# Squares of x summed in PSUM, Sin and Tanh emitted elsewhere, and the first merge weights loaded ahead of x

## The chip, the cores and the metric

The kernel runs on one core of a Trainium2 chip. The metric is the device time of one execution in microseconds, as a median of runs. TensorE (PE) multiplies matrices and has its weight loads listed apart (PEld), VectorE (DVE) does elementwise work, ScalarE (ACT) activations and copies, GpSimd (POOL) elementwise work too, and SyncE (SP) issues the DMA transfers. Each engine executes its own instructions in order.

## What is computed

One layer of an encoder over 1024 positions with 1024 channels, all in float32:

```
h    = rms_norm(x, g)
proj = h @ w_in                      # latent columns, RWKV columns, gate columns
o_a  = mla_branch(...)               # attention; rotary cos/sin of positions on q and k
o_b  = rwkv7_branch(...)             # uses tanh(low-rank decay columns), sigmoid(...)
x    = x + (sig(gA) * (o_a @ w_o[:512]) + sig(gB) * (o_b @ w_o[512:])) @ w_merge
x    = x + gated_mlp(rms_norm(x))
```

What the change touches is the root mean square of `x` over its channels, `cos` and `sin` of `positions * frequency`, the `tanh` of the two decay columns, and the product with `w_merge` together with the addition of `x` behind it.

## The kernel before

Everything is held transposed: 128 channels on the partitions, 1024 positions along the free axis, two halves of 512 (`HT`). A float32 product is made of three products in a reduced type: each operand is split into a high part (a cast on ACT) and a low part (a subtraction on DVE or POOL), and high x high, high x low and low x high are added in PSUM. `mmk` (L295) emits these six products, three for each half; this is called a step. `split` (L211) makes the parts of a weight tile: the cast `whi` on ACT, the subtraction `wlo` on POOL.

**The order of work.** The instructions of TensorE stand in the order in which the program emits them (L248). For DVE, ACT, POOL and SP, in the first part and around the merge, a scheduler of the language chooses the order from its own model of time; program order counts as priority. `act` (L152) adds ordering edges so that ScalarE's table sets are loaded in the order of emission: Ln and Exp share a set, Sigmoid and Tanh share one, Sin has its own.

**The start (L304 to L405).** `XORDER` (L42) lists the steps of the start: "w" loads and splits half of a weight tile of one of the first three projections (two for the latent q, one for the latent kv), "x" loads one of eight row blocks of x (`ld`, L322: hh on ACT, hl on DVE), "m" is one step of product, "q" squares a row block (`square`, L328: Square on ACT in place, then an addition into `acc` on POOL), "r" makes the rotary tables (`rotary_tables`, L340), and "s" sums the squares over the partitions with a product of `acc` by ones and takes the reciprocal root `rstd` by Ln and Exp on ACT. In TensorE's order "s" stands behind the two q products and ahead of the last four steps of the kv product. The rotary tables are 17 DVE instructions over 128 x 1024 and two Sin on ACT; they use the tiles `ang`, `kq`, `sinT` and `cosT`. `evac` (L400) then multiplies the three results by `rstd`, which empties their PSUM banks.

**The projections behind it (L436 to L761).** `inproj` emits eight steps of one projection and calls `done` behind the last. The first two are l2 and l1 (L752). `shift` (L449) evacuates one into the single tile `u` and mixes each position with its neighbours (Identity on ACT, two DVE instructions); then `l1_done` and `l2_done` (L703, L707) apply Tanh to one half of the tile. Two lanes of background work (L719) are woven between the steps: generators such as `norm_ckv` and `norm_cq` (normalisations, L480), `key_rope` (L507, with the sum rsk), `mla_nope` and `rw_prep` (L637, for each of four pairs: three low-rank products from l1 and l2 with a Sigmoid behind each half). A generator that yields a key goes on after so many estimated nanoseconds of TensorE work as `DELAY` (L57) says for it, so this table sets where its products stand in TensorE's order.

**The merge (L1659 to L1733).** After the branches are mixed, the eight row blocks of x are loaded into `x2[j]` (L1659), held by an ordering edge behind the last gate load. Then, for each j, `product` (L1377) takes two weight tiles of 512 columns of `w_merge[j]`, from the list `first` if it holds any and otherwise by a load at that place, and makes eight steps; `residual` (L1709) adds `x2[j]`, and several ACT and DVE instructions scale, split and square the sum. Raw weight tiles, high parts and low parts have two buffers each.

Of the kernel before, what the change touches and what calls it, by code (L numbers as in the profile page):

```python
# [10 lines left out]
F32 = mybir.dt.float32  # L11
R = mybir.dt.float32r
I32 = mybir.dt.int32
# [41 lines left out]
CARRY = 3000  # L55
BATCH = 2500
DELAY = {  # L57
    "tab": 2100, "sum": 3900, "cq": 2040, "kr": 3100, "kr2": 750, "kr3": 0, "nope": 2975, "nope2": 1440,
    "rope": 541, "rope2": 5334, "rope3": 1470, "v": 805, "lora": 746, "kk": 10600, "kk2": 1785, "rk": 4080,
    "bo": 400,  # L60
}
# [25 lines left out]
def block_kernel(ctx: ExitStack, tc: tile.TileContext, a):  # L87
# [44 lines left out]
    def pool(name, bufs=1, side="left", space=bass.MemoryType.SB):  # L132
        return tc.tile_pool(name=name, bufs=bufs, side=side, space=space, reuse_waits="tile")
# [137 lines left out]
    onef = ap_.tile([128, 128], F32, name="onef")  # L271
    G.memset(onef, 1.0)
    G.tensor_copy(onesr, onef)
    HT = (slice(0, 512), slice(512, 1024))

    nst = [0]
# [27 lines left out]
    cqps = [big(), big()]  # L304
    ckps = [up1(), up1()]
    first3 = [*cqps, ckps]
    with pool("xp") as xp:
        xt = [xp.tile([128, T], F32, name=f"xt{k}") for k in range(8)]
        acc = xp.tile([128, T], F32, name="xacc")
        w3 = {}  # L310

        def wl3(t, h):
            raw = xp.tile([128, 512], F32, tag=f"raw{t}", name=f"raw{t}{h}")
            nc.sync.dma_start(raw, a["w_in"][t][:, h * 512:(h + 1) * 512])
            if h == 0:
                hi, lo = (xp.tile([128, 512], R, name=f"{n}{t}") for n in ("whi", "wlo"))
            else:
                hi, lo = (wpool["w"].tile([128, 512], R, tag=n, name=n, bufs=2) for n in ("whi", "wlo"))
            split(raw, hi, lo)
            w3[t, h] = hi, lo  # L320

        def ld(k):  # L322
            nc.sync.dma_start(xt[k], a["xT"][k * 128:(k + 1) * 128, :])
            hh, hl = hx[k]
            S.activation(hh, xt[k], AF.Copy, scale=vc("gmix", k))
            V.scalar_tensor_tensor(out=hl, in0=xt[k], scalar=vc("gmix", k), in1=hh.bitcast(F32), op0=mult, op1=sub)

        def square(k):  # L328
            if k == 0:
                S.activation(acc, xt[0], AF.Square)  # L330
            else:
                S.activation(xt[k], xt[k], AF.Square)
                G.tensor_tensor(out=acc, in0=acc, in1=xt[k], op=add)

        def mm(t, k):
            wh, wl = w3[t, k // 4]
            ws = slice(k % 4 * 128, (k % 4 + 1) * 128)
            mmk(first3[t], wh[:, ws], wl[:, ws], hx[k], k == 0, k == 7)

        def rotary_tables():  # L340
            posi = xp.tile([128, T], I32, name="posi")
            nc.sync.dma_start(posi, a["pos"].to_broadcast([128, T]))
            ang, kq = (xp.tile([128, T], F32, name=n) for n in ("ang", "kq"))
            V.tensor_copy(ang, posi)
            V.tensor_scalar(ang, ang, cst[:, C_FREQ:C_FREQ + 1], None, op0=mult)
            magic = 12582912.0
            for dst, off, fin in ((sinT, 0.0, 0.0), (cosT, 0.25, 0.5 * math.pi)):
                V.tensor_scalar(kq, ang, 1.0 / (2 * math.pi), off, op0=mult, op1=add)
                V.tensor_scalar(kq, kq, magic, -magic, op0=add, op1=add)
                src = ang  # L350
                rest = 2 * math.pi
                for bits in (8, 8, 8, 24):
                    if bits == 24:
                        cc = float(np.float32(rest))
                    else:
                        m, e = math.frexp(rest)
                        cc = math.ldexp(math.floor(m * 2 ** bits), e - bits)
                    rest -= cc
                    V.scalar_tensor_tensor(out=dst, in0=kq, scalar=-cc, in1=src, op0=mult, op1=add)
                    src = dst  # L360
                pi_ = 3.1415925
                if fin:
                    V.tensor_scalar(dst, dst, fin, pi_, op0=add, op1=ALU.min)
                    V.tensor_scalar(dst, dst, -pi_, None, op0=ALU.max)
                else:
                    V.tensor_scalar(dst, dst, pi_, -pi_, op0=ALU.min, op1=ALU.max)
                act(dst, dst, AF.Sin)

        for step in XORDER:
            if step[0] == "w":  # L370
                wl3(step[1], step[2])
            elif step[0] == "x":
                ld(step[1])
            elif step[0] == "q":
                square(step[1])
            elif step[0] == "r":
                rotary_tables()
            elif step[0] == "m":
                mm(step[1], step[2])
            else:  # L380
                for hs in HT:
                    ss = ss1()
                    E.matmul(ss, onef, acc[:, hs], start=True, stop=True)
                    rsqrt_(rstd[:, hs], ss, 1.0 / D, eps)
# [9 lines left out]
    def keep(i, n, dtype=F32):  # L394
        return tt(n, RV[i], 1, dtype)
# [4 lines left out]
    def evac(q, ps):  # L400
        for x, hs in zip(ps, HT):
            V.tensor_tensor(out=q[:, hs], in0=x, in1=rstd[:, hs], op=mult)

    for q, ps in zip([*cqs, ckv], first3):
        evac(q, ps)  # L405

    nc.sync.dma_start(a2w, a["w_l1"])
    for dst, src in ((b64r, a["consts"][:, C_B64:]), (b16, a["b16"])):
# [40 lines left out]
    def shift(ps, i, out):  # L449
        u = tt("u", "u", 1)  # L450
        evac(u, ps)
        S.activation(out, u, AF.Identity, scale=c0[:, i:i + 1])
        V.scalar_tensor_tensor(out=out[:, 1:], in0=u[:, :-1], scalar=vc("mp", i), in1=out[:, 1:], op0=mult, op1=add)
        V.scalar_tensor_tensor(out=out[:, :-1], in0=u[:, 1:], scalar=vc("mn", i), in1=out[:, :-1], op0=mult, op1=add)
# [25 lines left out]
    def norm_cq():  # L480
        sq = [tt("sq") for _ in range(2)]
        for i in range(2):
            S.activation(sq[i], cqs[i], AF.Square)
        G.tensor_tensor(out=sq[0], in0=sq[0], in1=sq[1], op=add)
        pt = parted2(sq[0])
        yield "sum"
        rs = tt("rs")
        for x, hs in zip(pt, HT):
            rsqrt_(rs[:, hs], gsum(onesr, x), 1.0 / 256, eps)
        for i in range(2):  # L490
            V.scalar_tensor_tensor(out=cqs[i], in0=cqs[i], scalar=vc("gqa", i), in1=rs, op0=mult, op1=mult)
            split(cqs[i], cqh[:, i, :], cql[:, i, :], V)
        yield "cq"
# [143 lines left out]
    def rw_prep(p):  # L637
        cs = slice(p * 128, (p + 1) * 128)
        w2b = tp.tile([64, 128], F32, tag="w2b", name="w2b", bufs=2)
        nc.sync.dma_start(w2b, a["w_l2"][:, cs])  # L640
        at = keep(3, "at")
        for dst, wt, src, bias, key in (
            (at, a2w[0:64, cs], l1[0:64, :], vc("a0", p), None),
            (None, a2w[64:128, cs], l1[64:128, :], vc("w0f", p), "s0"),
            (None, w2b, l2[0:64, :], vc("w0b", p), "s1"),
        ):
            if dst is None:
                dst = tt("sg")
            for hs in HT:
                ps = up1()  # L650
                mul(ps, wt, src[:, hs], start=True, stop=True)
                act(dst[:, hs], ps, AF.Sigmoid, bias=bias)
                yield "lora"
            if key:
                nc.sync.dma_start(d_rw[key][:, p, :], dst)
# [46 lines left out]

    def l1_done(ps):  # L703
        shift(ps, 0, l1)
        act(l1[64:128, :], l1[64:128, :], AF.Tanh)

    def l2_done(ps):  # L707
        shift(ps, 1, l2)
        act(l2[0:64, :], l2[0:64, :], AF.Tanh)

    def gl_done(d):
        def done(ps):
# [943 lines left out]
    for j in range(2, 8):  # L1656
        for _ in mixture(j):
            pass
    for j in range(8):  # L1659
        i = nc.sync.dma_start(x2[j][:, :], a["xT"][j * 128:(j + 1) * 128, :])  # L1660
        tc.add_manual_dep(i.ins, fetched[0].ins.name, NOSYNC, reason="after the branch's operands")

# [48 lines left out]
    for j in range(7):  # L1713
        ps = big4()
        for _ in product(ps, a["w_merge"][j], yx):
            pass
        if j == 6:
            first.extend([wrows(a["w_merge"][7], k, 8) for k in (0, 4)])
        residual(j, ps)
        k, g = j % 4, vc("gffn", j)  # L1720
        y1, y2_ = ps
        scaled((B11 if j < 4 else B21)[k], y1, g)
        if j < 4:
            d = t5("p1")
            S.copy(d, y1)
            V.tensor_tensor(out=d, in0=y2_, in1=d, op=sub)
            scaled(U1[k], d, g)
        else:
            t3, t2 = sums(j, ps, scaled_b12(j))
            split(t3, *U3[k], V)  # L1730
            split(t2, *U2[k], V)
            scaled(B22[k], y2_, g)
        squares(j, ps)  # L1733
# [461 lines left out]
```

## Time and profile before

| | |
|---|---|
| median of 3 runs | 1922.2 us (1920.16 to 1922.29) |
| profiled execution | 1920.34 us |
| its span | 1918.4 us |
| mean granted TensorE clock | 0.978 |
| busy PE / DVE / ACT / POOL | 1832.6 / 1220.6 / 871.5 / 654.1 us |
| DMA | 210.65 MB, mean 110 GB/s |

Times in the profile count from the start of the span. A line of the timeline has start, duration, engine, line of the program, operation, output and inputs by tile name, shape, and how many instructions were put together; in brackets stands how long the engine had been idle and what released it. Nearly all instructions are recorded in two helpers (L108, and L123 for TensorE), so they are told apart by their tiles. The ends of products are modelled: where products follow each other closely, the distance between starts is what one takes.

### The profile page before, as it was taken

What the parts mean: (1) busy time and instruction counts of PE and PEld (TensorE: products, weight loads), DVE (VectorE), ACT (ScalarE), POOL (GpSimd) and SP (SyncE); (2) the same over time, 40 slices, a digit from 0 to 9 for tenths busy, and PEclk for the clock granted to TensorE, in tenths of its full rate; (3) what the DMA queues carried; (4) which work ended last, traced back from release to release, by engine and by line L of the source; (5) the groups of instructions that cost most, each with busy time, mean ns of one, the idle gap of its engine ahead of it and who ended that gap; (6) DMA issues with size and microseconds to landing.
All of it is one profiled execution on the core that took longest, in us unless ns stands there. A gap on an engine that the chain in (4) does not pass through costs nothing. (4 is left out here: it accounts for less than half of the span.)

```text
span 1918.4 us, 36770 instructions
## 1 busy us (share of the span) xinstructions
PE 1832.6 (96%) x14928; PEld 1464.1 (76%) x14928; DVE 1220.6 (64%) x1853; ACT 871.5 (45%) x1390; POOL 654.1 (34%) x566
## 2 busy tenths in 40 slices
PE   6889999999999998998999999999999999999998
PEld 5657676888788776776777877877888888888886
DVE  7567665445466586776673363697666766667667
ACT  5576577223232565665666543543323323333231
POOL 7435553521222324252533322246222232222221
PEclk9899999999999998998999999999999999999999
DMA  4135644854464644444433681211111111111112
GB/s 160 33 121 185 189 167 148 251 136 103 122 167 116 153 111 129 114 119 96 110 92 132 205 319 67 66 44 44 61 56 50 50 50 62 54 50 50 51 54 104
DMA packets 260632, 210.65 MB, mean 110 GB/s; under 512 B 127144, under 2 KB 205032, under 8 KB 260464
## 3 DMA queue, kind: packets, MB, share of 16 engines
q1 hardware_dynamic: 260464, 208.31, 36.7%
q8 instruction: 117, 1.92, 0.4%
q14 instruction: 51, 0.42, 0.1%
HBM read 144.64 MB, written 59.41 MB: 106 GB/s over the span
## 5 line engine op out<-in xcount | busy, mean ns | idle before, releaser
L108 POOL TENSOR_TENSOR wlo<-wraw,whi 128x512 fp32r<-128x512 f32 x118 | 159.8, 1354 | 589.3 <-ACT whi L108 569.9
L123 PE MATMUL st<-hh,whi 128*128 128x512 f32 x408 | 171.5, 420 | 14.1 <-ACT hh L108 8.9
L123 PE MATMUL st<-hl,whi 128*128 128x512 f32 x408 | 163.1, 400 | 0.7 <-DVE hl L108 0.7
L108 DVE TENSOR_TENSOR x<-b,x 128x512 f32<-128x512 f32 x176 | 119.1, 686 | 55.8 <-PE b L123 55.8
L123 PE MATMUL st<-hh,wlo 128*128 128x512 f32 x408 | 139.9, 397 | 0.5 <-POOL wlo L108 0.5
L108 POOL TENSOR_TENSOR pl<-pe,ph 128x512 fp32r<-128x512 f32 x64 | 82.9, 1298 | 162.6 <-ACT ph L108 144.2
L108 ACT CAST whi<-wraw 128x512 fp32r<-128x512 f32 x118 | 73.0, 619 | 126.4 <-issue 32.3
L123 PEld LDWEIGHTS st<-hh,whi 128*128 128x128 f32 x408 | 78.3, 192 | 41.0 <-issue 9.6
L108 DVE TENSOR_REDUCE mx<-sc 128x1 f32<-128x512 f32 x128 | 81.8, 682 | 27.5 <-PE sc L123 27.4
L123 PEld LDWEIGHTS st<-hh,wlo 128*128 128x128 f32 x408 | 78.2, 192 | 18.5 <-POOL wlo L108 1.1
L123 PEld LDWEIGHTS st<-hl,whi 128*128 128x128 f32 x408 | 78.8, 193 | 17.6 <-DVE hl L108 1.7
L108 POOL TENSOR_TENSOR wl<-wraw,wh 128x512 fp32r<-128x512 f32 x22 | 28.9, 1313 | 173.1 <-ACT wh L108 163.3
L108 DVE TENSOR_TENSOR u<-b,p 128x512 f32<-128x512 f32 x42 | 29.0, 690 | 70.6 <-PE b L123 70.6
L123 PE MATMUL b<-sh,wh 128*128 128x512 f32 x176 | 69.9, 397 | 2.2 <-ACT sh L108 2.2
L123 PE MATMUL b<-sl,wh 128*128 128x512 f32 x176 | 69.7, 396 | 0.5 <-DVE sl L108 0.5
L123 PE MATMUL b<-sh,wl 128*128 128x512 f32 x176 | 69.5, 395 | 0.0
L123 PE MATMUL b<-sh,whi 128*128 128x512 f32 x176 | 68.6, 390 | 0.3 <-DVE x L108 0.3
L123 PE MATMUL b<-sl,whi 128*128 128x512 f32 x176 | 68.5, 389 | 0.0
L123 PE MATMUL b<-sh,wlo 128*128 128x512 f32 x176 | 68.5, 389 | 0.0
L108 DVE TENSOR_TENSOR pl<-st,ph 128x512 fp32r<-128x512 f32 x64 | 43.6, 683 | 28.3 <-ACT st L108 27.9
L108 ACT CAST whi<-s 128x512 fp32r<-128x512 f32 x33 | 20.6, 623 | 87.2 <-PE b L123 87.2
L123 PE MATMUL po<-ph,vhh 128*128 128x512 f32 x128 | 58.0, 453 | 1.8 <-ACT rc L108 1.8
(487 smaller groups left out, 5344.8 us busy)
## 6 DMA issues: line engine op xcount, KB each, us to landing
wraw<-w_in SPq DMA_DIRECT2D x64, 256.0 KB
wraw<-w_fd SPq DMA_DIRECT2D x44, 256.0 KB
AA<-w_fu SPq DMA_DIRECT2D x41, 256.0 KB
A<-w_fg SPq DMA_DIRECT2D x41, 256.0 KB
ld<-d_x SPq DMA_DIRECT2D x32, 256.0 KB
d_gate<-gt SPq DMA_DIRECT2D x32, 256.0 KB
xt<-xT SPq DMA_DIRECT2D x8, 512.0 KB
d_s<-sg SPq DMA_DIRECT2D x8, 512.0 KB
```

The costliest lines, as they stand in the source:

```text
L108: return f(*args, **kw)
L123: return f(out, a, b, **kw)
```

## The change

The squares: the first goes from ACT straight into two PSUM tiles (`accps`), the others stay in place, and DVE adds them in PSUM, half by half; the last addition writes `acc`. Each Square becomes the group behind which `act` orders the next table load. The positions are loaded into the space of `cosT`. The angles are computed behind the evacuation of the first three projections, with `l1` and a tile of another pool as scratch; the two Sin stand at the head of `l2_done`. The two Tanh move from `l1_done` and `l2_done` into `rw_prep` of the first pair, with a delay "tanh" of 2500 behind them. `norm_cq` gets a delay of its own, "cq0" of 9500, in place of "sum", 3900. In the merge, both weight tiles of `w_merge[0]` are loaded before any row of x, and row j + 1 of x is loaded behind the product j.

```diff
 DELAY = {
-    "tab": 2100, "sum": 3900, "cq": 2040, ...
+    "tab": 2100, "cq0": 9500, "tanh": 2500, "sum": 3900, "cq": 2040, ...
...
+    posi = cosT.bitcast(I32)
...
+    accps = [ss1(), ss1()]
...
         def square(k):
-            if k == 0:
-                S.activation(acc, xt[0], AF.Square)
-            else:
-                S.activation(xt[k], xt[k], AF.Square)
-                G.tensor_tensor(out=acc, in0=acc, in1=xt[k], op=add)
+            if k:
+                cur["group"] = [S.activation(xt[k], xt[k], AF.Square)]
+            for hs, p in zip(HT, accps):
+                if k == 0:
+                    S.activation(p, xt[0][:, hs], AF.Square)
+                else:
+                    V.tensor_tensor(out=p if k < 7 else acc[:, hs], in0=p, in1=xt[k][:, hs], op=add)
...
             elif step[0] == "r":
-                rotary_tables()
+                nc.sync.dma_start(posi, a["pos"].to_broadcast([128, T]))
...
     for q, ps in zip([*cqs, ckv], first3):
         evac(q, ps)
+
+    def rotary_tables():
+        ang, kq = l1, keep(3, "kq")
+        V.tensor_copy(ang, posi)
...
+    rotary_tables()
...
             S.activation(sq[i], cqs[i], AF.Square)
         G.tensor_tensor(out=sq[0], in0=sq[0], in1=sq[1], op=add)
         pt = parted2(sq[0])
-        yield "sum"
+        yield "cq0"
...
         at = keep(3, "at")
+        if p == 0:
+            for x, r in ((l1, slice(64, 128)), (l2, slice(0, 64))):
+                act(x[r, :], x[r, :], AF.Tanh)
+            yield "tanh"
...
     def l1_done(ps):
         shift(ps, 0, l1)
-        act(l1[64:128, :], l1[64:128, :], AF.Tanh)
 
     def l2_done(ps):
+        for dst in (sinT, cosT):
+            act(dst, dst, AF.Sin)
         shift(ps, 1, l2)
-        act(l2[0:64, :], l2[0:64, :], AF.Tanh)
...
-    for j in range(8):
+    first.extend([wrows(a["w_merge"][0], k, 8) for k in (0, 4)])
+
+    def load_x(j):
         i = nc.sync.dma_start(x2[j][:, :], a["xT"][j * 128:(j + 1) * 128, :])
         tc.add_manual_dep(i.ins, fetched[0].ins.name, NOSYNC, reason="after the branch's operands")
+
+    load_x(0)
...
         for _ in product(ps, a["w_merge"][j], yx):
             pass
+        load_x(j + 1)
```

More of the change, by code (lines that the diff above doesn't have):

```diff
@@ L57 @@
 DELAY = {
-    "tab": 2100, "sum": 3900, "cq": 2040, "kr": 3100, "kr2": 750, "kr3": 0, "nope": 2975, "nope2": 1440,
+    "tab": 2100, "cq0": 9500, "tanh": 2500, "sum": 3900, "cq": 2040, "kr": 3100, "kr2": 750, "kr3": 0, "nope": 2975, "nope2": 1440,
     "rope": 541, "rope2": 5334, "rope3": 1470, "v": 805, "lora": 746, "kk": 10600, "kk2": 1785, "rk": 4080,
@@ L338, in mm @@
             mmk(first3[t], wh[:, ws], wl[:, ws], hx[k], k == 0, k == 7)
[L340 to L367, printed above, removed]
         for step in XORDER:
@@ L405, in block_kernel @@
         evac(q, ps)
+    def rotary_tables():
+        ang, kq = l1, keep(3, "kq")
+        V.tensor_copy(ang, posi)
+        V.tensor_scalar(ang, ang, cst[:, C_FREQ:C_FREQ + 1], None, op0=mult)
+        magic = 12582912.0
+        for dst, off, fin in ((sinT, 0.0, 0.0), (cosT, 0.25, 0.5 * math.pi)):
+            V.tensor_scalar(kq, ang, 1.0 / (2 * math.pi), off, op0=mult, op1=add)
+            V.tensor_scalar(kq, kq, magic, -magic, op0=add, op1=add)
+            src = ang
+            rest = 2 * math.pi
+            for bits in (8, 8, 8, 24):
+                if bits == 24:
+                    cc = float(np.float32(rest))
+                else:
+                    m, e = math.frexp(rest)
+                    cc = math.ldexp(math.floor(m * 2 ** bits), e - bits)
+                rest -= cc
+                V.scalar_tensor_tensor(out=dst, in0=kq, scalar=-cc, in1=src, op0=mult, op1=add)
+                src = dst
+            pi_ = 3.1415925
+            if fin:
+                V.tensor_scalar(dst, dst, fin, pi_, op0=add, op1=ALU.min)
+                V.tensor_scalar(dst, dst, -pi_, None, op0=ALU.max)
+            else:
+                V.tensor_scalar(dst, dst, pi_, -pi_, op0=ALU.min, op1=ALU.max)
+    rotary_tables()
     nc.sync.dma_start(a2w, a["w_l1"])
```

## The prediction, made before the changed kernel was run

> **What bounds the kernel now.** I read the span by stages first, then TensorE's timeline in the stages where it idles, then the engine that each wait names, then the chain of waits around the merge.
>
> ```profile
> 0.00:41.80 41.80, 31.36 (x120) 23.73 (x120) 31.67 (x22) 23.70 (x26) 29.99 (x19) 1.00 0.51 183
> 41.80:61.40 19.60, 10.25 (x28) 6.61 (x28) 15.11 (x12) 6.94 (x10) 9.04 (x6) 0.76 0.09 23
> 61.40:91.20 29.80, 27.83 (x104) 22.04 (x105) 11.63 (x12) 18.53 (x25) 13.97 (x9) 0.87 0.12 36
> 91.20:122.60 31.40, 23.95 (x76) 13.85 (x75) 25.09 (x22) 24.42 (x34) 10.85 (x8) 0.89 0.23 65
> 137.00:300.00 163.00, 156.79 (x616) 113.10 (x614) 111.07 (x114) 108.86 (x154) 86.71 (x57) 0.99 0.53 175
> ```
>
> Columns are the stage, its length, busy time of PE, PEld, DVE, ACT and POOL, the granted clock, DMA share and GB/s. TensorE (PE) is the bound: from 137 us on it is busy 96% at full clock. Between 41.8 and 122.6 it idles and runs at 0.76 to 0.89 of the clock. Its waits there:
>
> ```profile
> 28.70 0.39 PE L123 MATMUL st<-hh,whi 128*128 128x512 f32 x1
> 41.21 0.39 PE L123 MATMUL po<-hh,wlo 128*128 128x512 f32 x1
> 46.12 3.78 PE L123 MATMUL ss<-xacc,onef 128*128 128x512 f32 x4 [4.52 <-POOL xacc L108]
> 61.45 0.80 PE L123 MATMUL st<-hh,whi 128*128 128x512 f32 x1 [5.08 <-DVE cq L108]
> 64.18 0.63 PE L123 MATMUL st<-hh,whi 128*128 128x512 f32 x1
> 66.22 0.39 PE L123 MATMUL st<-hh,whi 128*128 128x512 f32 x1
> 67.58 0.39 PE L123 MATMUL st<-hh,whi 128*128 128x512 f32 x1
> 70.30 0.40 PE L123 MATMUL ss<-phi,onesr 128*128 128x512 f32 x1
> 71.23 0.39 PE L123 MATMUL st<-hh,whi 128*128 128x512 f32 x1
> 75.32 0.39 PE L123 MATMUL st<-hh,whi 128*128 128x512 f32 x1
> 82.46 0.64 PE L123 MATMUL ss<-plo,onesr 128*128 128x512 f32 x1 [1.46 <-POOL plo L108]
> 91.20 0.39 PE L123 MATMUL st<-hh,whi 128*128 128x512 f32 x1
> 103.05 0.80 PE L123 MATMUL ss<-ghi,b64r 128*128 128x512 f32 x1 [5.02 <-ACT rsk L108]
> 106.70 1.12 PE L123 MATMUL up<-l,a2w 64*128 64x512 f32 x2
> 121.98 0.50 PE L123 MATMUL up<-ckh,shi 128*128 128x512 f32 x1 [2.43 <-ACT sg L108]
> ```
>
> A step of a projection is six products; warm it takes 1.36 us (66.22 to 67.58), the first step after a pause 2.73 (61.45 to 64.18). The second pause stands behind ScalarE (ACT), which holds the two Sin ahead of the reciprocal root:
>
> ```profile
> 46.65 1.06 ACT L108 ACTIVATE sinT<-sinT 128x1024 f32<-128x1024 f32 x1 [9.93 <-DVE sinT L108]
> 56.52 1.06 ACT L108 ACTIVATE cosT<-cosT 128x1024 f32<-128x1024 f32 x1 [7.78 <-DVE cosT L108]
> 57.59 1.28 ACT L108 ACT_TABLE_LOAD   x1
> 58.89 1.27 ACT L108 ACTIVATE rstd<-ss,cst 128x512 f32<-128x512 f32 x2
> 99.95 1.05 ACT L108 ACTIVATE l<-l 64x1024 f32<-64x1024 f32 x1 [2.45 <-DVE l L108]
> 101.02 1.28 ACT L108 ACT_TABLE_LOAD   x1
> 102.31 1.25 ACT L108 ACTIVATE rsk<-ss,cst 64x512 f32<-64x512 f32 x2
> ```
>
> The sums that the root needs were ready at about 50, yet ACT sat until cosT's angle came. The last three rows are the same pattern with a Tanh. VectorE (DVE) is slow because GpSimd (POOL) works beside it:
>
> ```profile
> L108 DVE SCALAR_TENSOR_TENSOR hl<-xt,vec,hh x8: 1283/3363/3435, 8.9 to 30.0; 128x1024 fp32r<-128x1024 f32 x8
> L108 POOL TENSOR_TENSOR xacc<-xacc,xt x7: 2848/3267/3340, 14.0 to 42.9; 128x1024 f32<-128x1024 f32 x7
> 33.34 0.74 DVE L108 TENSOR_SCALAR ang<-ang,cst 128x1024 f32<-128x1024 f32 x1
> L108 DVE SCALAR_TENSOR_TENSOR sinT<-kq,sinT x3: 1366/1370/3274, 37.8 to 40.6; 128x1024 f32<-128x1024 f32 x3
> 43.90 2.71 DVE L108 TENSOR_SCALAR sinT<-sinT 128x1024 f32<-128x1024 f32 x1
> L108 DVE TENSOR_TENSOR b<-b,x x16: 687/694/700, 1163.9 to 1240.7; 128x512 f32<-128x512 f32 x16
> ```
>
> The three durations are minimum, median and maximum in ns. The merge, much later, has one pause of its own:
>
> ```profile
> 1138.60 1.30 POOL L108 TENSOR_TENSOR wlo<-wraw,whi 128x512 fp32r<-128x512 f32 x1 [6.61 <-ACT whi L108]
> 1144.22 10.73 DMA wraw<-w_merge
> 1151.52 0.61 PE L123 MATMUL b<-yh,wlo 128*128 128x512 f32 x2
> 1155.73 0.80 PE L123 MATMUL b<-yh,whi 128*128 128x512 f32 x1 [3.59 <-ACT whi L108]
> 1163.91 0.39 PE L123 MATMUL b<-yh,whi 128*128 128x512 f32 x1
> 1163.88 1.30 DVE L108 TENSOR_TENSOR b<-b,x 128x512 f32<-128x512 f32 x2 [13.53 <-PE b L123]
> 1174.76 1.30 DVE L108 TENSOR_TENSOR b<-b,x 128x512 f32<-128x512 f32 x2 [5.67 <-PE b L123]
> ```
>
> **Squares in PSUM.** Seven POOL additions of 3.27 us go; DVE gets fourteen half-wide ones with one operand in PSUM. The nearest row is the residual addition, also PSUM with SBUF, 0.69 us: 14 x 0.69 = 9.7. The eight hl fall to their minimum, 8 x 1.28 = 10.3. DVE needs 20.0 us from its first hl at 8.9 and has the sum at about 29, where POOL gave it at 46. TensorE needs it when its two first products are done: from 28.70 to 41.44 it spent 12.7 us on eight steps worth 10.9, so at best 39.6. Ten us of slack cover waits for x. I take 1 of those 1.9 us as gained.
>
> That rests on the additions not being slowed as hl was (3.36 beside POOL's 3.27). The Trainium skill ("SBUF — State Buffer", section "Who interferes with whom") gives DVE and GpSimd one exclusive shared port pair, which a DVE instruction with two SBUF inputs needs and one with a single SBUF input, outside the two-port modes, does not. By it the additions cost 9.7 us even beside POOL; the hl rows agree for two SBUF inputs, and no row here has the other kind beside POOL.
>
> The other bound, from the hl row alone: a half-wide addition at half of 3.36, 1.7 us, 24 us in all; the sum would come at about 43 and TensorE pause 4 us.
>
> **Rotary tables and Sin behind the evacuation.** From 41.44 to 61.45 TensorE does 4 sum products (3.78 us at half clock, so 1.9 warm) and four steps (5.4): 7.3 of 20.0, 12.7 lost. Now: sums at 39.6, four ACT instructions of about 0.6 after the first half give the root at 43, two evacuations of 0.69 free the first banks at 44.4, and TensorE is busy with the third product until 39.6 + 1.9 + 5.4 = 46.9. Nothing is waited for, provided that ACT holds no Sin and DVE no long queue of angles ahead. One angle instruction in front costs up to 3.3. I take 11.7 of the 12.7.
>
> The angles still cost DVE what they did: from 33.34 to 56.5 they took 23.2 us. They now fill DVE's pauses before and behind the evacuations, and Sin comes behind the l2 projection. What is queued behind them: on DVE the shift of l2; on ACT, behind a Sin that waits, the casts of the next weights. The position broadcast now lands in cosT's space, at the same place of SP's queue; nothing reads it before the angles.
>
> **The two projections l2 and l1**, 61.45 to 91.20: sixteen steps (21.8) and eight sum products (0.93 for four, so 1.9) make 23.7 of 29.75, 6.1 lost: 2.0 by the slow clock (two steps in 4.77 instead of 2.72), the rest at the sums that wait for POOL plo and slow products behind them. The clock stays warm now, and the later "cq0" puts those sums four steps (5.4 us) further back, which covers the 1.46. Against that stand ACT's waits at Sin. I take 3 of 6.1.
>
> **Tanh moved**, 91.20 to 122.6: ACT no longer stands 2.45 us at l plus a table load of 1.28 and a Tanh of 1.05 ahead of rsk, which TensorE awaited 5.02 us and then ran eight products in 3.65 (103.05 to 106.70) instead of 1.8: 6.9 in all. I take 5; the 2.43 at 121.98 I leave. The "tanh" delay sets the six low-rank products two steps (2.7 us) back in the written order; their first result meets a key projection that ends some 30 us later, so I cost this at nothing, at 2.7 without that cover.
>
> The Trainium skill ("TensorE: Matmul & The Clock Gate", Part 1) lets the clock fall only after an idle window of about 3.4 us. The trace disagrees: after 1.46 us of idle the product at 82.46 ran 0.64. By the page the waits that I leave would cost no clock. By the row they cost up to 2 us more each, which is in my shortfalls.
>
> **Merge weights ahead of x.** The weights for the second half of the first merge product were issued at 1144.22, behind 4 MB of x, and arrived 10.73 us later; their raw buffer had been free since 1138.60 + 1.30 = 1139.90. Issued then, even with the slowest flight, 10.73, they land at 1150.6, cast and low part (0.6, ACT's price for this size in the rstd row, and 1.3) at 1152.5, against TensorE's need at 1152.0; without x in front they should land about 5 earlier. The pause and its slow clock: 1152.0 to 1163.91 holds four steps (5.4), so 11.9 - 5.4 = 6.5 lost. I take 6.5. Rows of x are needed one per 10.9 us (1163.88 to 1174.76) and each is issued a product ahead; I cost them at nothing, at up to 5 once, behind the last product, if the cover went.
>
> **Sum.** 1 + 11.7 + 3 + 5 + 6.5 = 27.2 us. The profiled execution is 1920.3 (span 1918.4 and 1.9 around it), so 1893. The median of the runs shown is 1.9 above that execution, the lowest 0.2 below. After 137 us DVE and ACT are under 70% busy and nothing is tied to absolute time, so a shift of the front should arrive at the end.
>
> **Rivals.** (a) ACT stands at Sin with the weight casts behind it. If DVE takes the angles only after the last evacuation (48.2) and needs 23.2, cosT's Sin ends at 72.5 and the second half of l1's weights is ready at 75, not at 46.9 + 16.3 = 63.2: 11.8 and 2 of slow clock, of which 3.1 is in my sum. Total gain 16.5, 1904. For: that is how 9.93 and 7.78 arose. Against: the angles' inputs are there early, and POOL's load beside them falls. Chance 0.20.
> (b) The merge weights still stand behind x, since the scheduler orders SP: gain 20.7, 1900. Against: they come first in the program and their buffer is free early. 0.07.
> (c) Only the merge gains, because engines behind the front, 68% busy DVE above all, fill up and give it back by 300 us: 1914. Against: TensorE leads there. 0.06.
> (d) Slower: all of l1's casts stand behind Sin and DVE is slowed throughout. Eight angle instructions at 3.27 and nine at 2.71 are 51 us, so cosT is ready at 99, and l1 starts 3 us later at 102 instead of 75.32. That loses 27 against 5 + 6.5 and the vanished plo wait of 4: 1931. It decides from an angle time of about 40 us on (ready at 88). Against: POOL would have to work beside every instruction, and 22.4 us of its load (7 x 3.2) are gone. 0.04.
> My forecast keeps 0.63.
>
> **Range.** Low end: all front losses recovered, 1.9 + 12.7 + 6.1 + 9.3 + 6.5 = 36.5, and 2 more of the 6.2 idle us between 137 and 300: 1881. High end: (a) with 3 us for the unmeasured additions, 1907. This leaves out (c) and (d) and some tails. Measurement tells this kernel apart within about 0.2%, 3.8 us: faster 0.94, same 0.02, slower 0.04.
>
> **What would show it.** Right: hl near 1.3 us; no PE wait on POOL for the sum; rstd on ACT at about 41 with both Sin after it; the l2 projection starting near 47, the projection behind l1 (91.20 before) near 72; no wait above 1 us at the first merge product. Wrong: ACT idle before cosT's Sin with TensorE waiting on whi behind it, or x ahead of w_merge on SP.

## The result, and the profile after

| | before | after |
|---|---|---|
| median of the runs | 1922.24 us (1913.99 to 1928.36, 14 runs) | 1908.34 us (1902.57 to 1915.09, 14 runs) |
| ratio, 95% interval | | 0.9929, 0.9912 to 0.9946 |
| profiled execution, its span | 1920.34, 1918.4 us | 1902.57, 1900.8 us |
| granted clock | 0.978 | 0.985 |

The change gains 13.6 us by the ratio (13.9 between the medians); 27.2 us, and so a time of 1893, were forecast. The profiled execution of after is the fastest of its 14 runs, 5.8 us below their median, so the two traces differ by 17.8 us, more than the kernels do. The stages of after, by the same windows view as before:

```profile
0.00:39.30 39.30, 30.17 (x121) 24.17 (x122) 22.44 (x31) 23.25 (x28) 10.43 (x14) 1.00 0.54 195
39.30:46.20 6.90, 6.90 (x29) 5.09 (x28) 4.75 (x7) 2.85 (x6) 2.00 (x3) 1.00 0.21 67
46.20:72.50 26.30, 24.09 (x105) 19.17 (x103) 25.99 (x20) 16.43 (x22) 14.84 (x9) 1.00 0.09 31
72.50:102.50 30.00, 25.63 (x76) 14.98 (x76) 25.84 (x24) 25.95 (x37) 11.83 (x9) 0.89 0.26 78
122.00:286.00 164.00, 153.76 (x600) 109.93 (x599) 103.33 (x110) 105.59 (x151) 86.77 (x57) 0.99 0.51 172
```

The first three rows are what was forecast: the stage of the sums and the root, 19.60 us long before, is 6.90 long with TensorE never idle, and the two projections behind it take 26.3 us instead of 29.8, at full clock. The last row is not: TensorE idles 10.2 us of 164 where it idled 6.2 of 163. Its timeline (left out between the lines are unbroken products):

```profile
46.18 0.39 PE L123 MATMUL st<-hh,whi 128*128 128x512 f32 x1
...
72.52 0.50 PE L123 MATMUL st<-hh,whi 128*128 128x512 f32 x1 [1.69 <-ACT whi L108]
...
74.30 0.80 PE L123 MATMUL st<-hh,wlo 128*128 128x512 f32 x2 [0.58 <-POOL wlo L108]
...
91.87 1.12 PE L123 MATMUL up<-l,a2w 64*128 64x512 f32 x2 [1.85 <-ACT at L108]
...
94.60 0.50 PE L123 MATMUL ss<-glo,b64r 128*128 128x512 f32 x1 [1.18 <-POOL glo L108]
...
102.87 0.50 PE L123 MATMUL up<-ckh,shi 128*128 128x512 f32 x1 [1.12 <-ACT sg L108]
...
151.50 0.50 PE L123 MATMUL ss<-glo,b64r 128*128 128x512 f32 x1 [2.61 <-POOL glo L108]
...
161.40 0.50 PE L123 MATMUL ss<-glo,b64r 128*128 128x512 f32 x1 [1.15 <-POOL glo L108]
```

The l2 projection starts at 46.18 (61.45 before), the one behind l1 at 72.52 (91.20). The pause of 5.02 us at rsk is gone. But from 91 us on there are pauses that the kernel before did not have, most of them at a sum whose low part POOL has yet to make. The waits view (TensorE) shows how much of the idle time of the last stage that is, first after (122 to 286), then before (137 to 300); columns are the sum in us, the number and the longest:

```profile
PE ss L123 <- POOL glo L108: 6.9, 5, 2.6
PE ss L123 <- POOL glo L108: 1.4, 2, 0.8
```

ScalarE's timeline at the front, and VectorE's:

```profile
40.03 0.69 ACT L108 ACTIVATE rstd<-ss,cst 128x512 f32<-128x512 f32 x1 [0.65 <-PE ss L123]
...
59.21 1.06 ACT L108 ACTIVATE sinT<-sinT 128x1024 f32<-128x1024 f32 x1
60.18 0.60 ACT L108 CAST whi<-wraw 128x512 fp32r<-128x512 f32 x1
...
69.48 1.06 ACT L108 ACTIVATE cosT<-cosT 128x1024 f32<-128x1024 f32 x1 [1.58 <-DVE cosT L108]
70.56 1.28 ACT L108 ACT_TABLE_LOAD   x1
71.85 0.62 ACT L108 CAST whi<-wraw 128x512 fp32r<-128x512 f32 x1
```

```profile
41.42 1.29 DVE L108 TENSOR_TENSOR cq<-st,rstd 128x512 f32<-128x512 f32 x2 [9.38 <-ACT rstd L108]
```

The root comes at 40.03 with both Sin behind it. The cast that TensorE awaits at 72.52 stands behind cosT's Sin and a table load: rival (a) of the prediction, in small (2.27 us). VectorE meanwhile sat idle for 9.38 us ahead of the evacuation with most of the angles still to do, queued behind it. The merge, by SP's queue, then ACT, then TensorE:

```profile
1128.23 0.33 SPq L220 DMA_DIRECT2D wraw<-w_merge  x1
1128.62 0.42 SPq L1669 DMA_DIRECT2D x<-xT  x1
1129.15 0.37 SPq L1651 DMA_DIRECT2D y<-d_y  x1
1129.57 5.75 SPq L1669 DMA_DIRECT2D x<-xT  x7
1136.36 24.85 SPq L220 DMA_DIRECT2D wraw<-w_merge  x6
```

```profile
1146.93 1.27 ACT L108 CAST whi<-wraw 128x512 fp32r<-128x512 f32 x2 [8.47 <-DMA wraw<-w_merge]
```

```profile
1147.60 0.50 PE L123 MATMUL b<-yh,whi 128*128 128x512 f32 x1 [1.19 <-ACT whi L108]
```

Both tiles of the first product's weights went ahead of x, and its pause is gone. But the rows of x did not go one per product: the scheduler, which orders SP, sent all eight ahead of the second product's weights, and there a smaller pause arose. One more, far behind anything the change touches:

```profile
616.09 2.43 PE L123 MATMUL sc<-Un,NM 16*32 16x16 f32 x128 [1.06 <-DMA Un<-dU]
618.45 0.80 PE L123 MATMUL st<-hh,whi 128*128 128x512 f32 x1
619.04 0.63 PE L123 MATMUL st<-hl,whi 128*128 128x512 f32 x1
```

**The lead.** All kernels here have 14,928 products on TensorE. The lead is the start of the n-th product in the kernel before, less that in the other kernel. With the tanh delay at 2500 the order differs between products 218 and 1161 (79 to 340 us), so that the column 137 there compares work done, not the same product. Columns are the time in the kernel before, in us; "again" is a second profiled execution of the changed kernel, the other names are those of the experiments.

```
               62    137    341    600    650   1090   1175   1900
after        15.6   19.4   14.1   14.5    9.9   11.8   15.7   17.9
again        15.0   18.4   11.5   13.0    9.0    0.4    6.0    8.2
e13_un       15.1   18.3   11.5   13.2   14.2   10.3   15.2   17.4
e1_front     14.7   18.0   12.7   15.7   10.2    7.2    8.7   10.9
e4_held      14.5   16.7   11.4   11.7    7.8   -1.4    5.0    5.1
e11_port     14.7   17.8   12.5   13.1    8.8    3.5    8.3   10.5
e3_tanh0     14.1   16.2   16.4   17.9   18.2   16.2   20.5   22.5
e8_sinfirst  16.0   19.2   19.3   20.9   20.3   15.1   18.4   20.4
e9_realign   15.8   19.8   18.3   20.6   20.3   19.1   24.9   27.0
e10_evac     14.5   19.6   19.8   19.7   20.4   20.2   25.8   27.9
e12_best     15.9   20.5   19.1   20.8   18.9   15.5   20.5   22.6
e5_squares    6.8    4.2    5.8    8.0    8.5    2.6    3.9    6.0
e6_rotary    12.9    8.1    6.7    8.4    6.2    3.9    3.2    2.9
e7_tanh      -0.2    3.5   -3.5   -2.6   -2.9   -4.1   -5.0   -5.0
e2_merge      0.1   -0.8   -0.7    0.3    0.3   -0.4    4.7    6.7
```

Single executions differ by 2 to 3 us in the front and by more behind 650, so groups of rows are to be read, not one against another.

### The profile page after: what moved, and what is told of

Read it like the earlier page. It is cut to its first block, busy times and chain, and to the rows that moved or that the text cites. A ratio compares the mean times of both kernels' runs of the same rounds, so it can differ in the third digit from the quotient of the medians.

```text
span 1900.8 us, 36763 instructions
## 1 busy us (share of the span) xinstructions
PE 1821.6 (96%) x14928; PEld 1457.5 (77%) x14928; DVE 1214.8 (64%) x1867; ACT 865.6 (46%) x1387; POOL 634.1 (33%) x559
## 5 line engine op out<-in xcount | busy, mean ns | idle before, releaser
L108 POOL TENSOR_TENSOR wlo<-wraw,whi 128x512 fp32r<-128x512 f32 x118 | 164.1, 1391 | 564.0 <-ACT whi L108 561.7
L123 PEld LDWEIGHTS st<-hh,whi 128*128 128x128 f32 x408 | 77.9, 191 | 37.3 <-issue 10.4
L108 DVE TENSOR_REDUCE mx<-sc 128x1 f32<-128x512 f32 x128 | 81.9, 683 | 27.2 <-PE sc L123 27.0
```

The source lines that it names most:

```text
L108: return f(*args, **kw)
L123: return f(out, a, b, **kw)
```

## The experiments

Two questions were open: what the merge edit is worth, and why a front that led by 18 to 19 us at 137 us leads by 11 to 14 at 341 and by 9 to 10 at 650.

**The merge taken apart.** The changed kernel with the old loop over the eight rows of x (e1_front), and the kernel before with the merge edit alone (e2_merge):

```diff
-    first.extend([wrows(a["w_merge"][0], k, 8) for k in (0, 4)])
-    def load_x(j):
+    for j in range(8):
...
-    load_x(0)
...
-        load_x(j + 1)
```

> The front of the change alone; the merge as before. Theory T1 (the merge edit gave about 4.5 us: it removed the pause of the first merge product, 6.5 us, and made a new one of 1.9 us at the second): slower than the changed kernel by 4 to 5 us, ratio to before about 0.995. TensorE shows the old wait of 3.6 us at the first merge product. Rival T2 (the merge edit gave nothing that lasts; the whole gain is the front's): same time as the changed kernel, ratio 0.993.

> The merge edit alone, the front as before. T1: 4 to 5 us faster than before, ratio 0.9977, with a wait of 1 to 2 us at the second merge product, whose weights stand behind the eight rows of x. T2: no difference that can be measured, ratio 1.000.

e1_front: 1911.51 us, ratio 0.9954 (0.9936 to 0.9972). e2_merge: 1919.02 us, 0.9982 (0.9961 to 1.0003). By time alone e2_merge does not exclude that the edit gives nothing. The leads do, taken together: from 1090 to 1175 the eleven executions with the merge edit gain 3.3 to 6.4 us, the four with the old loop -0.9 to 1.5 (e1_front, e5_squares, e6_rotary, e7_tanh). The edit is worth some 4 to 5 us. TensorE's waits fit T1 in e1_front (3.44 us at the first product); in e2_merge the wait at the second product is 0.45 us, less than the 1 to 2 expected.

**The rows of x held** behind the latest weights, which makes SP send one row and two weight tiles in turn:

```diff
         tc.add_manual_dep(i.ins, fetched[0].ins.name, NOSYNC, reason="after the branch's operands")
+        tc.add_manual_dep(i.ins, wpool["load"].ins.name, NOSYNC, reason="after the weights")
```

> The changed kernel with each row of x held on SP behind the merge weights that the program loads before it, so that the rows really go one at a time. T1: the wait at the second merge product (1.2 us by its own record, 1.9 us with the slow clock behind it) is gone and no row comes late: 1.9 us faster than the changed kernel, which this measurement can hardly tell in the time but the lead over the kernel before, product by product, shows (6.5 us gained over the merge instead of 4.5). Rival: a row that comes late at the residual addition takes its place; lead over the merge 4.5 or less.

1910.46 us, ratio 0.9940 (0.9916 to 0.9964): no difference in time from the changed kernel. SP now alternates, TensorE has no pause at the first or the second product, and the lead rises by 6.4 us from 1090 to 1175, the forecast's 6.5. The 2.2 us that other executions gain later, at the head of the gated MLP (the column 1900 against 1175), are missing here; e6_rotary and e7_tanh miss them too, without this edit, and e12_best, which has it, gains them, so that they are not its price.

**The delay at nothing.** The changed kernel with one number changed:

```diff
-    "tanh": 2500,
+    "tanh": 0,
```

> The changed kernel with the delay behind Tanh set to 0, so that TensorE's written order behind the first two projections is that of the kernel before again (only the four sums of the latent q stay four steps later). Theory A (the front's lead of 25 us was given back because the delay of 2500 re-wrote the order of TensorE and set sums closer behind the parts that POOL makes): the lead at 340 us is 20 us or more in place of 14.2, in spite of one wait of about 3 us for Tanh at the first low-rank product; time about 5 us under the changed kernel. Theory B (the engines beside TensorE, POOL and DVE above all, cannot work faster, whatever the order): the lead at 340 us is 14 to 15 us again, time within 2 us of the changed kernel.

1899.69 us, ratio 0.9885 (0.9862 to 0.9907): 8.6 us below the changed kernel. TensorE's order is then that of before, but for four sum products. The lead is 16.2 at 137 and 16.4 at 341: nothing is given back. The expected 20 was missed. The wait of about 3 us that it had at the first low-rank product did not come there, but one of 2.77 at ACT's Sigmoid behind them (104.57 us, 2.43 at 121.98 in before). And this execution leads by only 14.1 at 62 us already; e8_sinfirst below, with the same order, has 16.0 there and 19.3 at 341.

**The delay by itself.** The kernel before with both Tanh moved and the delay of 2500:

```diff
+    "tanh": 2500,
...
+        if p == 0:
+            for x, r in ((l1, slice(64, 128)), (l2, slice(0, 64))):
+                act(x[r, :], x[r, :], AF.Tanh)
+            yield "tanh"
...
-        act(l1[64:128, :], l1[64:128, :], AF.Tanh)
...
-        act(l2[0:64, :], l2[0:64, :], AF.Tanh)
```

> The kernel before with both Tanh moved into rw_prep of the first pair and the delay of 2500 behind them, nothing else: no engine is ahead of where it was at 90 us. Theory A (the delay re-writes TensorE's order up to 340 us, and that order costs 4 us there and 4 more at the late operand Un near 620 us): a lead of about 5 to 7 us at 114 us, 0 to 2 at 340, and a pause at the first product with Un that the kernel before does not have; time 1919 to 1925, ratio 0.998 to 1.002. Rival B (the order has no price, the lead was eaten because a TensorE that runs 20 us ahead catches up with the engines that feed it): the 5 us stay, time about 1917, ratio 0.997 or less.

1925.02 us, ratio 1.002 (1.000 to 1.0039). Nothing is early here, and yet the lead falls from 7.1 at 114 us to -3.5 at 341, more than theory A expected, with the same pauses at glo as in the changed kernel (2.61 and 1.15):

```profile
167.41 0.50 PE L123 MATMUL ss<-glo,b64r 128*128 128x512 f32 x1 [2.60 <-POOL glo L108]
...
177.31 0.50 PE L123 MATMUL ss<-glo,b64r 128*128 128x512 f32 x1 [1.12 <-POOL glo L108]
```

That excludes rival B, that a TensorE 20 us ahead catches up with its suppliers: here it is ahead of nothing at 91 us (-0.9) and waits just as long. The expected pause at Un did not come; see e13_un.

**The delay kept, the rest put back.** The low-rank products stay two steps later, but the delay behind each is cut, so that what is written behind them stands where it stood:

```diff
-    "tanh": 2500,
+    "tanh": 2500, "lora0": 330,
...
-                yield "lora"
+                yield "lora" if p else "lora0"
```

> The changed kernel with its tanh delay of 2500, and the delay behind each of the six low-rank products of the first pair cut from 746 to 330: those products still come two steps later, but everything written behind them in TensorE's order stands where it stands with the delay at 0. Theory A (it is the shift of all the work behind, up to 340 us, that cost the lead): the lead at 137 us is 18 to 20, at 340 the same, no pause at the first product with Un, time 1895 to 1898. Rival B2 (setting the low-rank products back is itself what costs): the lead falls to about 13 at 340 as in the changed kernel, time about 1908.

1899.55 us, ratio 0.9862 (0.9838 to 0.9886). The lead is 19.8 at 137 and 18.3 at 341. The waits at 91 to 103 us are the changed kernel's, to 0.03 us; those behind are before's. TensorE's busy time in the stage behind, for e9_realign, e3_tanh0 and e7_tanh:

```profile
121.00:285.00 164.00, 157.80 (x609) 112.34 (x607) 109.95 (x112) 107.39 (x152) 86.70 (x57) 0.98 0.54 177
```

```profile
121.00:284.00 163.00, 156.86 (x616) 113.08 (x615) 110.91 (x114) 108.48 (x154) 86.72 (x57) 0.99 0.54 175
```

```profile
137.00:300.00 163.00, 152.65 (x593) 109.24 (x591) 103.14 (x110) 102.52 (x146) 86.71 (x56) 0.98 0.51 170
```

TensorE idles 6.2 and 6.1 us with the old order behind (6.2 in before, without the front), and 10.4 (10.2 in the changed kernel and in its second execution) with the shifted one. So it is not the Tanh and not the six products that cost, but the shift of everything written behind them. The expected 1895 to 1898 was missed by 1.6 us.

**The parts of the front.** The kernel before with the squares in PSUM alone (e5_squares: `square`, `accps` and nothing else of the diff), and with the angles and both Sin moved alone (e6_rotary: `rotary_tables`, `posi` and the two lines in `l2_done`):

> The kernel before with the squares in PSUM alone: angles, both Sin and both Tanh stand where they stood, so the reciprocal root still waits for cosT's Sin on ACT. Theory P (the front was gained by taking Sin away from in front of the root): VectorE is free of POOL at about 31 us, the 17 angle instructions (eight of about 0.7 us, nine of about 1.25) end at about 49, Sin, the table load of 1.28 and the root follow, and the l2 projection starts at about 55.5 instead of 61.45, a lead of about 6 us; at 340 us a lead of 4 to 6, time about 1917. Rival Q (the front was gained by silencing POOL, and where the Sin stand matters little): a lead of 11 or more at the start of l2, time 1911 or less.

> The kernel before with the angles emitted behind the evacuation and both Sin at the head of l2_done, nothing else: POOL still adds the squares. Theory P: TensorE still waits about 4.5 us for the sum of the squares (46.12), but the root follows at about 49 and the l2 projection starts at about 52, a lead of about 9 us; then the angles, slowed where POOL works, come late, and 2 to 4 us are lost again behind the Sin. Time about 1915. Rival Q: a lead under 5 at l2, because the sum comes at 46 whatever is done about Sin, and VectorE remains slow; time 1918 or more.

e5_squares: 1914.93 us, ratio 0.9970 (0.9945 to 0.9994). ScalarE's timeline there:

```profile
49.71 1.06 ACT L108 ACTIVATE cosT<-cosT 128x1024 f32<-128x1024 f32 x1 [1.92 <-DVE cosT L108]
50.77 1.28 ACT L108 ACT_TABLE_LOAD   x1
52.07 1.27 ACT L108 ACTIVATE rstd<-ss,cst 128x512 f32<-128x512 f32 x2
```

The root still waits for cosT's Sin, which comes at 49.7 as theory P worked out, and l2 starts at 54.63 (55.5 expected). e6_rotary: 1916.77 us, ratio 0.9979 (0.9959 to 0.9999). Its lead at 62 is 12.9, more than the 9 expected, because the sum itself came sooner: with the angles gone from beside them, POOL's additions were done for TensorE at 41.66, not 46.12 (the last two took 4.86 us, not 6.62). Then 6 us are lost by 341, where 2 to 4 were expected. The two alone bring 6.8 and 12.9 at 62, together 15.6: in part both remove the same wait. Theory P holds at the start of l2, where moving the Sin is the larger part; at 341 the two are alike (5.8 and 6.7), and their times do not tell them apart.

In e6_rotary table loads stand between the root's own steps:

```profile
42.82 0.69 ACT L108 ACTIVATE rstd<-ss,cst 128x512 f32<-128x512 f32 x1 [0.39 <-PE ss L123]
43.53 1.28 ACT L108 ACT_TABLE_LOAD   x1
44.82 0.63 ACT L108 ACTIVATE rstd<-rstd 128x512 f32<-128x512 f32 x1
45.47 1.28 ACT L108 ACT_TABLE_LOAD   x1
```

The changed kernel has none there. The line with `cur["group"]` in the new `square`, which e6_rotary lacks, orders the next load behind the squares; that it is this line which keeps the loads out of the root is argued, not tried.

**VectorE's idle 9.4 us.** First by program order: the angle of sinT emitted ahead of the evacuation, tanh delay 0.

```diff
+    rotary_tables((sinT, 0.0, 0.0))
     for q, ps in zip([*cqs, ckv], first3):
         evac(q, ps)
-    rotary_tables()
+    rotary_tables((cosT, 0.25, 0.5 * math.pi))
```

> The changed kernel with the tanh delay at 0, and the angle of sinT emitted ahead of the evacuation (that of cosT behind it, as before). In the changed kernel VectorE sat idle for 9.4 us, from 32.0 to 41.4, while the angles stood behind the evacuation in its order; the weight cast behind cosT's Sin then held TensorE for 1.69 and 0.58 us at the projection behind l1. If that idle stretch is what the Sin were late for, both waits vanish and the lead over the kernel before at 340 us is 18 to 19 instead of 16.2: time 1897 or less against 1899.7. If the order puts the evacuation behind the angle, TensorE stands up to 2 us at the start of l2 and nothing is gained: 1899 to 1902.

1901.76 us, ratio 0.9896 (0.9864 to 0.9928). VectorE's order did not change, nor did the two waits (1.69 and 0.57): the scheduler goes by its own times before it goes by program order. The run says nothing on the idle stretch. It does give a second execution of e3_tanh0's order at the front: 19.3 against 16.4 at 341. Then by an ordering edge:

```diff
+            if angle:
+                tc.add_manual_dep(i.ins, angle[0].ins.name, NOSYNC, reason="the angle first")
```

> The changed kernel with the tanh delay at 0, and an ordering edge that puts the evacuation of the first three projections behind the angle of sinT on VectorE. Emitting the angle earlier had left VectorE's order as it was, idle for 9.3 us ahead of the root. The nine instructions of this angle take about 7 us undisturbed (four of about 1.25, the others about 0.7), so they end at about 39 of the 41 us at which the root comes: the evacuation should lose nothing, cosT's angle should end about 6 us earlier (near 63 instead of 69.4) and the two waits at the projection behind l1 (1.69 and 0.58) should vanish: a lead of 18 to 19 at 340 us against 16.2, time about 1897. Rival: the waits stay, since ACT has cosT's Sin behind sums and roots that do not move, and the time is that with the delay at 0, 1899 to 1902.

1890.57 us, ratio 0.9815 (0.9795 to 0.9835), the best of all. VectorE's timeline, then ACT's:

```profile
39.24 0.69 DVE L108 TENSOR_SCALAR sinT<-sinT 128x1024 f32<-128x1024 f32 x1
42.59 0.69 DVE L108 TENSOR_TENSOR cq<-st,rstd 128x512 f32<-128x512 f32 x1 [2.66 <-ACT rstd L108]
```

```profile
62.11 1.07 ACT L108 ACTIVATE cosT<-cosT 128x1024 f32<-128x1024 f32 x1 [0.67 <-DVE cosT L108]
63.20 1.28 ACT L108 ACT_TABLE_LOAD   x1
64.49 0.62 ACT L108 CAST whi<-wraw 128x512 fp32r<-128x512 f32 x1
```

The angle ended at 39.9, the evacuation lost nothing, cosT's Sin came 7.4 us earlier than in the changed kernel, and both waits are gone. At 96 us the lead is 19.1 against 16.2 and 16.5 in the two executions without the edge; at 105 it is 22.4 against 20.5 and 22.4, since a wait for rsk (0.91; 0.58 and none in those two) took part of it, and at 341 19.8 against 16.4 and 19.3. So of some 3 us gained at 96, between 0 and 2 are left at 105, and what there is at 341 (0.5 and 3.4) is about what those two differ by themselves (2.9). The rest of the 9 us between its median and e3_tanh0's arises behind 650, where the edit touches nothing, and is not explained.

**All together** (e9_realign, e10_evac and e4_held):

> Together: the realigned order of the low-rank products, the evacuation behind the angle of sinT, and the rows of x held behind the merge weights. If the three gains add: a lead of 20 or more at 340 us, no pause at the second merge product, time about 1894, ratio 0.985 to 0.987. If the held rows only move their loss to the head of the gated MLP, as the run with them alone had it: 1896.

1894.27 us, ratio 0.9831 (0.9808 to 0.9855). As expected in time, but not below e10_evac: 19.1 of lead at 341 where 20 or more were expected, no pause at the merge (5.0 from 1090 to 1175), and no proof that the three add.

**The additions beside POOL.** The changed kernel with POOL doing its seven additions again, into a spare tile that nobody reads:

```diff
                 cur["group"] = [S.activation(xt[k], xt[k], AF.Square)]
+                G.tensor_tensor(out=spare, in0=xt[0], in1=xt[k], op=add)
```

> The changed kernel with seven additions of 128x1024 on GpSimd into a spare tile beside the squares: POOL again does what it did before, for nothing, while VectorE adds in PSUM. By the rule of the page SBUF (one SBUF operand: no shared port) the PSUM additions stay at about 0.64 us each though POOL works beside them, and hl, with two SBUF operands, goes back to about 3.3. By the other bound of the prediction the PSUM additions rise to about 1.7 us each.

1909.86 us in one run. Minimum, median and maximum in ns, by tile:

```profile
L108 DVE TENSOR_TENSOR ss<-ss,xt x12: 679/682/684, 14.4 to 36.8; 128x512 f32<-128x512 f32 x12
```

```profile
L108 DVE SCALAR_TENSOR_TENSOR hl<-xt,vec,hh x8: 1286/2226/3425, 8.3 to 27.9; 128x1024 fp32r<-128x1024 f32 x8
```

```profile
L108 POOL TENSOR_TENSOR spare<-xt,xt x7: 2386/3261/3396, 13.7 to 38.3; 128x1024 f32<-128x1024 f32 x7
```

The PSUM additions take 0.68 us with POOL at work beside nearly all of them (0.683 in the changed kernel), while hl goes back to as much as 3.4, with a median of 2.2. That is the rule of the Trainium skill ("SBUF — State Buffer", "Who interferes with whom"): a DVE instruction with at most one SBUF input, outside the two-port modes, does not contend with GpSimd. The other bound of the prediction, 1.7 us each, is refuted.

**The pause at Un.** SP's queue in the changed kernel, then in e3_tanh0:

```profile
609.47 0.50 SPq L1221 DMA_DIRECT2D kh<-d_kh  x1
...
612.11 1.85 SPq L921 DMA_DIRECT2D Un<-dU  x4
```

```profile
604.09 2.15 SPq L921 DMA_DIRECT2D Un<-dU  x4
...
610.34 0.63 SPq L1221 DMA_DIRECT2D kh<-d_kh  x1
```

Ordering edges on SP put the four loads of Un of the scan's fourth round ahead of the attention's loads for its next head (for kh, qh, vhh and vhl alike; one is shown). The changed kernel is run again beside it:

```diff
             i = nc.sync.dma_start(dst.bitcast(F32), src)
+            if h == 1:
+                tc.add_manual_dep(i.ins, un[0].ins.name, NOSYNC, reason="after the scan's operand")
```

> The changed kernel with ordering edges that put the four loads of Un for the fourth round of the scan ahead of the attention's loads of its next head on SP, where the kernel with the tanh delay at 0 had them by itself. In the changed kernel they went out at 612.1, behind three of those loads, TensorE wanted Un at 615.0 and got it at 616.1, and the products behind ran at 0.63 us for some 12 us: a pause of 1.06 us that took 4.6 of the lead. If the place of these loads is the cause: no pause at the first product with Un, no slow products behind it, and the lead at 650 us equals that at 600 within 1 us; time about 4 us below the changed kernel, 1904. If the clock falls there whatever the loads do: the lead drops by 3 or more at 620 to 650 all the same, 1908.

> The changed kernel once more, unchanged: its first profiled execution was 5.7 us faster than its median. A lead of 11 to 13 us at 340 us and a pause at the first product with Un, as the four runs with this order had it; the rest of the gap to the median lost between 650 and 1100 us, where nothing of the change stands.

e13_un: 1904.69 us, ratio 0.9926 (0.9898 to 0.9953), where 1904 was expected. The median is 3.6 us below the changed kernel's, but the ratio is the same (0.9929), so the time does not decide, and whether these edges are worth anything at the end is not shown. The trace does: no wait at the first product with Un and no slow ones behind it, and the lead goes from 13.2 at 600 to 14.2 at 650.

```profile
616.34 1.26 PE L123 MATMUL sc<-Un,NM 16*32 16x16 f32 x128
617.53 0.50 PE L123 MATMUL st<-hh,whi 128*128 128x512 f32 x1
```

The same kernel without the edges, e14_again (1912.26 us in one run), lost 4.0 there and 8.6 more by 1090. All five executions of the shifted order with the front early and SP left alone lose 3.9 to 5.5 at that place, and no other kernel loses more than 2.2.

## Why the prediction was wrong

**It failed at the step of the "tanh" delay, costed at nothing.** The forecast asked only when the results of the six products themselves would be needed ("some 30 us later, so I cost this at nothing"). But the delay moves one lane of background work against the other, and everything written behind it changes place up to 340 us. That order has sums so close behind POOL's parts that TensorE idles 10 us instead of 6 between 122 and 286, and 1.2 us more from 286 to 322, where e3_tanh0 idles none: of 18 to 19 us at 137, 11 to 14 are left at 341 (e3_tanh0, e7_tanh, e9_realign show it from three sides). The price in time is 8.6 us, which is what the changed kernel lies above itself with the delay at nothing (1908.34 against 1899.69). With it went the last line under the sum, that a shift of the front should arrive at the end: in the old order the front's lead holds (e3_tanh0 leads by 16.2 us at 137 and by 18.2 at 650), in the shifted order it doesn't, though VectorE is no busier (64% in before and in after).

**SP's order far behind.** Also unforeseen: the scheduler sent Un's loads later. That costs 4 to 5 us of lead at 616 (e13_un). It came only where the early front and the shifted order were together: e7_tanh, e3_tanh0 and e9_realign have no such pause. Why the scheduler then chose so stays open.

**Step by step**, for the profiled execution of after:
- Squares, 1 forecast: the last product ahead of the sums starts at 38.75 instead of 41.21, 2.5 (the sum was there at 31.4, against 29 worked out); in e1_front, e3_tanh0 and e4_held 1.0 to 1.5. The choice of 0.69 per addition held (0.683, and 0.682 beside POOL).
- Sums and root, 11.7 forecast: 12.8 (l2 starts 15.3 earlier, less 2.5).
- l2 and l1, 3 forecast: 61.45 to 91.20 was 29.75, 46.18 to 72.52 is 26.34, 3.4. Rival (a) came true behind it with 2.27 us of wait, not 11.8: cosT's Sin was as late as that rival had it (done at 70.5 against 72.5), but ACT made the second cast for l1 at 60.18, between the two Sin, so that only the next projection's cast stood behind.
- Tanh, 5 forecast: the wait for rsk went, but ACT, with a table load and the Tanh ahead of the low-rank products' Sigmoid, now holds TensorE at 91.87 (1.85 us), and a wait for POOL (1.18) and slow products follow. From 18.7 at 91.20 the lead was 19.4 at 137, 0.7 gained; the same edit gains 4.4 in e7_tanh (-0.9 to 3.5), where nothing else is early. That the lead at 137 comes near the forecast all the same, 18 to 19 us against 20.7, is luck: terms 1 to 3 were 3.0 too small, this one 4.3 too large.
- Merge, 6.5 forecast: the pause at the first product and its slow products were taken away whole, but a new one of 1.19 us and the slow products behind it took 2 back: 4.5 (11.2 of lead at 1145, 15.7 at 1175). "Each is issued a product ahead" was wrong, since the scheduler sent all rows at once; e4_held, which forces it, gains 6.4.

In the mean of the two profiled executions of the changed kernel, the lead of 18.9 at 137 becomes 12.8 at 341, 9.5 at 650, 6.1 at 1090 and 13.1 at the end, beside a median gain of 13.9 (1922.24 less 1908.34).

**Left open.** Between 650 and 1090 the lead changes by -9.2 to +1.9 us in the shifted order and by -5.9 to -0.2 in the others, with no edit there. The executions of one kernel differ by almost as much (-8.6 and +1.9 for the changed one), so I do not explain it. The 2.2 us that most executions gain at the head of the gated MLP come from a slow stretch near 1298: in before, e4_held, e6_rotary and e7_tanh, 11 products behind a wait of 2.2 us take 0.63 us each. In the others such products stand ahead of that wait, which is then 0.6 us long, or there are none. The order of the products is the same, and why the clock falls here or there, or not at all, is open.

## What to carry to other kernels

A delay or an emission point in a hand-ordered program is not a local edit: compare the whole written order of the bound engine before and after, and realign what stands behind. Where a scheduler orders a queue, program order is a wish; look at the queue in the trace, and force with an edge what must hold. Time gained early was kept here only in an order whose products had their operands ready earlier too.

## What the runs showed of the hardware

- A wait of 1.06 us at 616.09, with 128 tiny products behind it, was followed by 13 us in which the large products were recorded at 0.63 us instead of 0.39, and 4.6 us of lead were lost, the wait among them. The windows view of after has the granted clock there as 0.65:

```profile
618.00:632.00 14.00, 14.00 (x284) 11.21 (x276) 4.35 (x9) 1.91 (x5) 0.00 (x0) 0.65 0.58 139
```

  The same tiny products without a wait (629.50 in before, 616.34 in e13_un) had none of that. The Trainium skill ("TensorE: Matmul & The Clock Gate", Part 1) asks for an idle window of about 3.4 us. The wait and the tiny products together take 3.4 us (615.03 to 618.45), so this place contradicts it only if such products count as work, which no run shows. The pauses of 1.69 and 0.58 us from 70.83 to 74.30 do contradict it: products run between them, and those from 74.90 on take 0.63 us.
- VectorE adding PSUM and SBUF is indifferent to POOL (0.682 us beside it, 0.683 without), whereas hl with two SBUF operands goes from 1.28 to as much as 3.4.
- POOL's seven useless additions cost the changed kernel nothing that one run shows (1909.86 against a median of 1908.34): VectorE has the sum of the squares at 38.7 us instead of 31.4, and TensorE, which takes it at 39.59, still does not wait.
